# First two token tiles normed with gains read from PSUM in halves, two idle products for seven, another early order of weights and tokens

## The chip, the cores and the metric

The kernel runs on one core of one Trainium2 chip. The metric is the device time of one execution in microseconds (us), lower is better. A core has five engines that work side by side and meet at semaphores: TensorE (PE in the profile, with its weight loads as PEld), VectorE (DVE), ScalarE (ACT), GpSimd (POOL) and SyncE (SP), which here issues nearly all DMAs. Each engine takes its instructions in the order of its own queue.

## The reference

One encoder block on 1024 tokens of width 1024, with 16 meta tokens put ahead of them. What matters here is its first step: an RMS norm with a gain per column, and the projection of the normed tokens by `w_in`.

```python
def rms_norm(x, g):
    xf = x.astype(jnp.float32)
    y = xf * lax.rsqrt(jnp.mean(xf * xf, axis=-1, keepdims=True) + EPS)
    return (y * g.astype(jnp.float32)).astype(x.dtype)
...
    h = jnp.concatenate([meta, x], axis=1)
    for layer in range(DEPTH):
        h = h + mixer_block(rms_norm(h, norm_mix[layer]), w_in[layer], ...)
        h = h + swiglu(rms_norm(h, norm_ffn[layer]), w_ff_gate[layer], w_ff_up[layer], w_ff_down[layer])
    return rms_norm(h, norm_final)[:, N_META:]
```

Inside `mixer_block` come the projection `h @ w_in`, differential attention (branch A of the reference), windowed attention (branch B, with the parts `qb`, `kb` and `vb` of the projection), gates and an output product. `swiglu` is a feed-forward part of width 2816.

## The kernel before

All products are made in two parts: a float32 operand is split into a rounded high part and a low part (the rest), and a product is the sum of high by high, high by low and low by high. `split` (L114) makes the two parts of a weight: ACT copies the high part (L115), and DVE or POOL subtracts it from the weight (L116).

**Tokens.** `load_x(t)` loads tile t of 128 tokens (x0 to x7, and the 16 meta tokens, tile NT). `norm_x(t)` calls `normed` (L130): ACT squares the tile and sums it (L133), POOL makes the reciprocal root in two small steps (L121, the mean, and L122, a power), and DVE multiplies tile, root and gain in one SCALAR_TENSOR_TENSOR of 128x1024 (L139). `turn_x(t)` calls `transposed` (L142): eight PE transposes by 128 columns into two PSUM banks (L148), and for each bank an ACT copy to the high part `hT_hi` (L150) and a DVE subtraction to the low part `hT_lo` (L151).

**Gains.** The gain is one row of 1024 numbers. PE transposes and spreads it over the partitions into two PSUM banks of 512 columns (L456), and DVE copies both to the tile `gmix` in SBUF (L457).

**Projection.** `project_steps` (L205) multiplies one block of 128 weight columns with a chunk of tokens: 8 steps (one for each 128 rows of the weight) of 3 products (L218). For the first chunk `hi_first` puts the eight high by high products ahead. The first blocks are `kb` (column C_KB) and the first two blocks of `qb` (q0 and q1); they go through four chunks of 256 tokens, the last of `kb` with the 16 meta tokens. So chunk 0 needs x0 and x1, chunk 1 needs x2 and x3, and so on. Their weights are loaded ahead: `preload(C_KB)`, `preload(C_QB)` (tile `w_c`, L179) and `w_q1` (L464). `ensure(n)` calls `prep`, which splits the next weight in the list `order` and loads it first if it isn't there; KB's low part is made on POOL, those of q0 and q1 on DVE.

**Buffers.** x tiles and `w_q1` share the tag `btr` with four buffers, so that x3 waits for x0's product (L139), x4 for x1's, and x5 for the low part of `w_q1`. Raw weights `w_c` have two buffers, so that the third (VB) waits for KB's low part.

**Idle products.** Products of a tile of zeros into a bank that nobody reads stand in PE's queue: eight at the start (L448), six behind the gain (L460), seven behind the transposes of x1 (L473). The last seven use a second tile of zeros that DVE makes from x0's normed tile (L471).

**Order.** The program is written as one sequence, and a planner lays it out: it simulates the engines, and at each engine issues the earliest in the program of those instructions that are ready by its own model of durations. The order in each queue is then fixed. `tc.issue_after(ins)` makes all instructions of its block that are on the engine of `ins` follow `ins` in that queue, without a wait for its end. `advance(n)` issues n steps from the list `early`, which holds the first chunks' projections; what is not issued by the calls in between comes in a last `advance(100)`, and so stands last in priority, but fills PE wherever it is ready first.

```python
    with tc.issue_after(high.ins):        # high: the last hT_hi copy of x0
        ensure(1)
    load_x(3)
    high, _ = turn_x(1)
...
    early += [(p_kb, DC), (p_q0, DC), (p_q1, DC)]
    advance(E_STEPS)
    norm_x(3)
    turn_x(2)
    advance(E_STEPS)
    load_x(4)
    norm_x(4)
    _, low = turn_x(3)
```

Of the kernel before, what the change touches and what calls it, by code (L numbers as in the profile page):

```python
# [73 lines left out]
def encoder_block(ctx: ExitStack, tc: tile.TileContext, x, meta, norm_mix, w_in, lq1, lk1, lq2, lk2,  # L74
# [22 lines left out]
    def bank(p, tag, name, bufs):  # L97
        return p.tile([P, 512], F32, tag=tag, name=name, bufs=bufs)
# [26 lines left out]
    def row(p, src, n, name):  # L125
        t = p.tile([P, n], F32, name=name, bufs=1)
        nc.sync.dma_start(t, src.broadcast_to([P, n]))
        return t

    def normed(p, src, parts, gain, name, tag="xn", bufs=2, on_pool=False):  # L130
        xn = p.tile([P, D], F32, tag=tag, name=f"xn_{name}", bufs=bufs)
        ss = small.tile([P, 1], F32, tag="ss", name=f"ss_{name}")
        nc.scalar.activation(xn[:parts], src, AF.Square, accum_out=ss[:parts])  # L133
        r = rstd_of(ss[:parts], D, parts, f"rstd_{name}")
        if on_pool:
            nc.gpsimd.tensor_scalar(xn[:parts], src, r[:parts], 1.0, ALU.mult, ALU.mult)
            nc.gpsimd.tensor_tensor(xn[:parts], xn[:parts], gain[:parts], ALU.mult)
        else:
            nc.vector.scalar_tensor_tensor(xn[:parts], src, r[:parts], gain[:parts], ALU.mult, ALU.mult)  # L139
        return xn  # L140

    def transposed(pp, xn, parts, hi, lo, at, name):  # L142

        for b in range(2):
            pt = pp(f"ptn_{name}_{b}").rearrange("p (c t) -> p c t", c=4)
            for c in range(4):
                k = 4 * b + c
                nc.tensor.transpose(pt[:, c, :parts], xn[:parts, k * P:(k + 1) * P], ident[:parts, :parts])  # L148
            h = hi[:, 4 * b:4 * b + 4, at:at + parts]
            high = nc.scalar.activation(h, pt[:, :, :parts], AF.Copy)  # L150
            low = nc.vector.tensor_tensor(lo[:, 4 * b:4 * b + 4, at:at + parts], pt[:, :, :parts], f32(h), ALU.subtract)  # L151
        return high, low

    acon, close_acon = pool("acon", "right")
    hpool, close_hpool = pool("hpool", "right")
# [254 lines left out]
    def load_x(t):  # L410
        xts[t] = bpool.tile([P, D], F32, tag="btr", name=f"x_{t}", bufs=4)
        if t < NT:
            nc.sync.dma_start(xts[t], x[t * P:(t + 1) * P, :])
        else:
            nc.sync.dma_start(xts[t][:NM], meta)

    def norm_x(t):
# [4 lines left out]
        xns[t] = normed(bpool, xts.pop(t)[:parts], parts, gmix, f"a{t}", tag=tag, bufs=bufs)  # L422

    def turn_x(t):
        parts = P if t < NT else NM
        return transposed(lambda name: bank(psum1, ("bt", "bs")[t % 2], name, 2), xns.pop(t), parts, hT_hi, hT_lo, t * P, f"a{t}")

    def advance(n):
        while n > 0 and early:
            g, left = early[0]  # L430
            next(g)
            n -= 1
            if left == 1:
                early.pop(0)
            else:
                early[0] = (g, left - 1)


    zeros = bpool.tile([P, 512], BF16, tag="by1", name="zeros", bufs=2)
# [9 lines left out]
    pt = bank(psum1, "bt", "gain_t", 2)  # L449
    nc.tensor.transpose(pt[:, 0:DC], rows, ident[:DC, :DC])  # L450
    nc.vector.tensor_copy(gain_t, pt[:, 0:DC])
    for b in range(2):
        pt = bank(psum1, "bs", f"gain_{b}", 2)
        for c in range(4):
            k = 4 * b + c
            turned = nc.tensor.transpose(pt[:, c * P:(c + 1) * P], gain_t[:, k:k + 1].broadcast_to([P, P]), ident)  # L456
        nc.vector.tensor_copy(gmix[:, b * 512:(b + 1) * 512], pt)  # L457
    with tc.issue_after(turned.ins):
        for _ in range(6):
            nc.tensor.matmul(idle, zeros[:, 0:P], zeros, start=True, stop=True)  # L460
# [1 line left out]
    preload(C_QB)  # L462
    w_q1 = bpool.tile([P, D], F32, tag="btr", name="w_q1", bufs=4).rearrange("p (c n) -> p c n", n=P)
    nc.sync.dma_start(w_q1, w_in[:, C_QB + P:C_QB + 2 * P].rearrange("(c p) n -> p c n", p=P))  # L464
    norm_x(0)
    load_x(2)
    norm_x(1)
    xn0 = xns[0]
    high, _ = turn_x(0)
    zeros = bpool.tile([P, 512], BF16, tag="by1", name="zeros", bufs=2)  # L470
    nc.vector.tensor_scalar(zeros, xn0[:, 0:512], 0.0, None, ALU.mult)  # L471
    for _ in range(7):
        nc.tensor.matmul(idle, zeros[:, 0:P], zeros, start=True, stop=True)  # L473
# [1081 lines left out]
```

## Time and profile before

| what | value |
|---|---|
| time, median of 3 runs | 1433.33 us (1432.73 to 1434.84) |
| the profiled execution's own time | 1433.01 us |
| its span, first to last instruction | 1430.9 us |
| PE busy | 1420.2 us, 99% of the span |
| DVE, ACT, POOL busy | 909.7, 673.3, 468.1 us |
| mean granted PE clock | 0.999 |

Times in the views count from the span's start. A row of the timeline gives the start, the length, the engine, the line, the operation, `out<-in`, the shape, the count xN of like instructions in a row, and in brackets how long the engine was idle ahead of it and what ended that. A row of the chain of waits gives start, length and what the chain ran through. A row of the table of stretches gives a stretch, its length, and the busy time of each engine (with the number of instructions), the granted clock, the busy share of the DMA engines and the GB/s. A queue name with q (SPq, ACTq) marks the issuing of DMAs, and the listing of DMA issues gives the time from issue to landing.

### The profile page before, as it was taken

The page shows a single profiled execution, that of the slowest core. Times are in us where ns is not written, and L with a number is a line of the kernel's source. Part 1 is how long each engine was busy: PE and PEld are TensorE (multiplying, and loading weights), DVE is VectorE, ACT ScalarE, POOL GpSimd, SP SyncE. Part 2 cuts the span into 40 slices and gives each one's busy share as a digit, 9 for nine tenths or more (in the row PEclk, how much of TensorE's full clock was granted, in tenths as well). Part 3 has the DMA queues.
Part 4 walks back from the last instruction along what each step waited for, and adds up shares of the span by engine and source line. Part 5 has one row for each costly group of instructions (what it writes and reads, how often), then busy time and mean ns, then how long its engine had stood idle before and what let it go on. Part 6 is the DMA issues. An engine that isn't in the chain of part 4 may idle for free.

```text
span 1430.9 us, 20933 instructions
## 1 busy us (share of the span) xinstructions
PE 1420.2 (99%) x7287; PEld 1222.8 (85%) x7287; DVE 909.7 (64%) x1807; ACT 673.3 (47%) x1276; POOL 468.1 (33%) x462
## 2 busy tenths in 40 slices
PE   8999999999999999999999999999999999999998
PEld 7998899988999999888788888888888888888886
DVE  7366566428686868446878966655544553787566
ACT  6355555425455555455346654333333333444454
POOL 5133233222323232212503044554545552000442
PEclk9999999999999999999999999999999999999999
DMA  7344333381524251087431724433332333954344
GB/s 230 91 123 116 100 113 96 90 253 56 149 75 149 75 156 68 30 297 253 132 134 75 207 87 141 152 99 111 103 102 99 101 103 103 352 192 140 126 125 148
DMA packets 159018, 191.55 MB, mean 134 GB/s; under 512 B 16104, under 2 KB 103600, under 8 KB 158912
## 3 DMA queue, kind: packets, MB, share of 16 engines
q1 hardware_dynamic: 158320, 189.15, 41.7%
q8 instruction: 58, 0.95, 0.3%
q10 hardware_dynamic: 592, 1.05, 0.2%
q14 instruction: 48, 0.39, 0.1%
HBM read 129.67 MB, written 53.94 MB: 128 GB/s over the span
## 4 chain that ended last, share of the span: by engine, by line
PE 94%; DVE 2%; DMA 1%; ACT 1%; POOL 1%; issue 0%; DVEq 0%; ACTq 0%
PE pg L1318 29%; PE pd L1422 14%; PE pp_g L218 12%; PE aps L692 4%; PE po L1221 4%; PE apy L734 3%; PE pp_ka L218 3%; PE pp_va L218 3%; PE pp_qa L218 3%; PE pp_qb L218 3%; PE ppa L636 3%; PE apt L721 2%; PE bps L349 2%; PE po L1229 2%; PE bpy L389 1%; PE bpt L384 1%
## 5 line engine op out<-in xcount | busy, mean ns | idle before, releaser
L1318 PE MATMUL pg<-t,wop 128*128 128x512 f32 x1056 | 242.4, 389 | 0.0
L1318 PEld LDWEIGHTS pg<-t,wop 128*128 128x128 f32 x1056 | 198.2, 188 | 41.2
L1422 PE MATMUL pd<-ob,oa 128*128 128x512 f32 x924 | 209.6, 389 | 0.0
L116 POOL TENSOR_TENSOR wop<-wf,wop 128x512 fp32r<-128x512 f32 x114 | 154.2, 1353 | 162.0 <-ACT wop L115 148.5
L1422 PEld LDWEIGHTS pd<-ob,oa 128*128 128x128 f32 x924 | 173.4, 188 | 36.0
L1318 PE MATMUL pg<-b,wop 128*128 128x512 f32 x792 | 183.3, 389 | 0.0
L1318 PEld LDWEIGHTS pg<-b,wop 128*128 128x128 f32 x792 | 148.4, 188 | 30.7
L116 POOL TENSOR_TENSOR wl_c<-w_c,wh_c 128x1024 fp32r<-128x1024 f32 x32 | 77.3, 2415 | 131.5 <-ACT wh_c L115 122.2
L115 ACT ACTIVATE wop<-wf 128x512 fp32r<-128x512 f32 x128 | 80.8, 632 | 73.7 <-PE pg L1318 44.3
L703 ACT ACTIVATE as<-as,amn 128x1040 f32<-128x1040 f32 x64 | 74.5, 1165 | 73.6 <-DVE amn L698 73.5
L218 PE MATMUL pp_g<-hT_hi,wh_c 128*128 128x512 f32 x256 | 100.8, 394 | 0.0
L218 PE MATMUL pp_g<-hT_lo,wh_c 128*128 128x512 f32 x256 | 100.4, 392 | 0.0
L218 PE MATMUL pp_g<-hT_hi,wl_c 128*128 128x512 f32 x256 | 100.3, 392 | 0.0
L115 ACT ACTIVATE oa<-ra 128x512 fp32r<-128x512 f32 x77 | 48.7, 632 | 108.5 <-PE pd L1422 50.4
L692 PE MATMUL aps<-ak,aq 128*128 128x352 f32 (+1 forms) x384 | 92.7, 326 | 0.0
L116 POOL TENSOR_TENSOR oa<-ra,oa 128x512 fp32r<-128x512 f32 x27 | 34.9, 1294 | 168.6 <-ACT oa L115 167.2
L1095 DVE TENSOR_TENSOR s<-wf,wf 128x512 f32<-128x512 f32 x22 | 16.9, 769 | 111.4 <-DMA wf<-in_w_ff_up_dram 70.0
L692 PEld LDWEIGHTS aps<-ak,aq 128*128 128x128 f32 x384 | 69.6, 188 | 13.8 <-issue 0.2
L698 DVE CUSTOM_DVE_ANT_0 as<-aps,dist,amn 128x352 f32<-128x352 f32 (+1 forms) x128 | 71.4, 563 | 10.4 <-PE aps L692 8.3
L361 POOL TENSOR_SCALAR bs<-bs,bdn 128x432 f32<-128x432 f32 (+1 forms) x64 | 37.0, 597 | 112.6 <-DVE bdn L359 99.0
L698 DVE CUSTOM_DVE_ANT_0 as<-aps,dist,far_a 128x352 f32<-128x352 f32 x64 | 37.1, 580 | 42.2 <-PE aps L692 42.0
L706 POOL TENSOR_SCALAR as<-as,adn,neglam 128x1040 f32<-128x1040 f32 x32 | 38.9, 1215 | 75.6 <-DVE adn L704 75.6
(290 smaller groups left out, 3044.1 us busy)
## 6 DMA issues: line engine op xcount, KB each, us to landing
ra<-aop SPq DMA_DIRECT2D x77, 256.0 KB, 2.6
w_c<-in_w_in_dram SPq DMA_DIRECT2D x33, 512.0 KB, 3.9
wf<-in_w_ff_gate_dram SPq DMA_DIRECT2D x25, 512.0 KB, 3.8
wf<-in_w_ff_up_dram SPq DMA_DIRECT2D x25, 512.0 KB, 3.8
aop<-as SPq DMA_DIRECT2D x44, 256.0 KB, 2.0
aop<-c SPq DMA_DIRECT2D x33, 256.0 KB, 2.0
g_d<-gate_stage SPq DMA_DIRECT2D x32, 256.0 KB, 2.0
gt<-g_d SPq DMA_DIRECT2D x32, 256.0 KB, 3.8
```

The source lines that it names most:

```text
L115: high = nc.scalar.activation(hi, src, AF.Copy)
L116: lo_eng.tensor_tensor(lo, src, f32(hi), ALU.subtract)
L218: product = nc.tensor.matmul(ps[:, :n], a[:, c, :], b[:, c, at:at + n], start=(u == 0), stop=(u == 3 * DC - 1))
L636: nc.tensor.matmul(ps, w[:, a, j, :], src(j, b, tk), start=(j == 0 and n == 0), stop=(j == 3 and n == 2))
L692: nc.tensor.matmul(ps[:, :n], qs[m][:, t * P:(t + 1) * P], ks[m][:, vv, k0:k0 + n], start=(vv == 0), stop=(vv == 1))
L698: nc.vector.tensor_tensor_reduce(s[m][:, a:b], ps[:, a - k0:b - k0], far_by, slope, low, ALU.add, ALU.min, mn[:, m, i + j:i + j + 1])
L703: nc.scalar.activation(s[m][:, 0:L], s[m][:, 0:L], AF.Exp, bias=low, scale=-1.0, accum_out=dn[:, m:m + 1])
L706: (nc.gpsimd if t % 4 in COMBINE_POOL else nc.vector).tensor_scalar(s[1][:, 0:L], s[1][:, 0:L], dn[:, 1:2], neglam, ALU.mult, ALU.mult)
L734: nc.tensor.matmul(py[:, cols], v[:kp, a, k, :], at_[:kp, k, b, :], start=(k == 0 and j == 0), stop=(k == 8))
L1221: nc.tensor.matmul(sets_o[p][u], oa[:, a, u * P:(u + 1) * P], ob[:, b, :], start=(p in (1, 5) and j == 0 and k == 0), stop=(p in (2, 3) an ...
L1318: nc.tensor.matmul(ps, op[:, x, c, :], b[:, y, c, :], start=(p in (1, 5) and c == 0 and n == 0), stop=(p in (4, 2, 3) and c == 3 and n == ...
L1422: nc.tensor.matmul(ps[u], oa[:, a, u * P:(u + 1) * P], ob[:, b, :], start=(p in (1, 2, 5) and j == 0 and k == 0), stop=(p in (2, 3, 4) and ...
```

## The change

The spread gain stays in its two PSUM banks until x0 and x1 are normed: for these two tiles DVE makes two products of 128x512, each with its half of the gain read from PSUM. The copies to `gmix` stay, ahead of x0's products on DVE; all later tiles use `gmix`. KB's weight is split behind the square of x1 on ACT, ahead of x0's high part. The idle products behind x1 go, with their tile of zeros; two that use the first zeros stand behind the transposes of x0. The steps of q1's chunk 0 come behind the transposes of x2, x4's product comes behind x2's low parts on DVE, chunk 0 and the first two steps of `kb`'s chunk 1 are issued ahead of x5, and x4's transposes come behind them. `transposed` returns all high copies and the last transpose, `advance` its last product.

```diff
+    squares = []
+
     def normed(p, src, parts, gain, name, tag="xn", bufs=2, on_pool=False):
...
-        nc.scalar.activation(xn[:parts], src, AF.Square, accum_out=ss[:parts])
+        squares.append(nc.scalar.activation(xn[:parts], src, AF.Square, accum_out=ss[:parts]))
...
+        elif isinstance(gain, list):
+            for i, half in enumerate(gain):
+                cols = slice(i * 512, i * 512 + 512)
+                nc.vector.scalar_tensor_tensor(xn[:parts, cols], src[:, cols], r[:parts], half[:parts], ALU.mult, ALU.mult)
         else:
             nc.vector.scalar_tensor_tensor(xn[:parts], src, r[:parts], gain[:parts], ALU.mult, ALU.mult)
...
+    gain = []
     for b in range(2):
         pt = bank(psum1, "bs", f"gain_{b}", 2)
+        gain.append(pt)
         for c in range(4):
             k = 4 * b + c
             turned = nc.tensor.transpose(pt[:, c * P:(c + 1) * P], gain_t[:, k:k + 1].broadcast_to([P, P]), ident)
-        nc.vector.tensor_copy(gmix[:, b * 512:(b + 1) * 512], pt)
+        copied = nc.vector.tensor_copy(gmix[:, b * 512:(b + 1) * 512], pt)
...
-    norm_x(0)
+
+    with tc.issue_after(copied.ins):
+        norm_x(0, gain)
     load_x(2)
-    norm_x(1)
-    xn0 = xns[0]
-    high, _ = turn_x(0)
-    zeros = bpool.tile([P, 512], BF16, tag="by1", name="zeros", bufs=2)
-    nc.vector.tensor_scalar(zeros, xn0[:, 0:512], 0.0, None, ALU.mult)
-    for _ in range(7):
-        nc.tensor.matmul(idle, zeros[:, 0:P], zeros, start=True, stop=True)
-
-    with tc.issue_after(high.ins):
+    norm_x(1, gain)
+    with tc.issue_after(squares[-1].ins):
         ensure(1)
+    _, _, turned = turn_x(0)
+    with tc.issue_after(turned.ins):
+        for _ in range(2):
+            nc.tensor.matmul(idle, zeros[:, 0:P], zeros, start=True, stop=True)
     load_x(3)
-    high, _ = turn_x(1)
+    highs, _, _ = turn_x(1)
     q1_h, q1_l = (bpool.tile([P, DC, P], F32R, tag=tag, name=f"{tag}_q1", bufs=1) for tag in ("wh", "wl"))
-    with tc.issue_after(high.ins):
+
+    with tc.issue_after(highs[-1].ins):
         ensure(2)
         high = split(q1_h, q1_l, w_q1, nc.vector)
...
-    early += [(p_kb, DC), (p_q0, DC), (p_q1, DC)]
+
+    def behind(steps, other):
+        for _ in range(DC):
+            with tc.issue_after(other.ins):
+                product = next(steps)
+            yield product
+
+    early += [(p_kb, DC), (p_q0, DC)]
     advance(E_STEPS)
     norm_x(3)
-    turn_x(2)
+    _, low, turned = turn_x(2)
+
+    early.append((behind(p_q1, turned), DC))
     advance(E_STEPS)
     load_x(4)
-    norm_x(4)
-    _, low = turn_x(3)
+    with tc.issue_after(low.ins):
+        norm_x(4)
+    _, low, _ = turn_x(3)
     early += [(p_kb, DC), (p_q0, DC), (p_q1, DC)]
-    advance(E_STEPS)
+
+    product = advance(3 * DC)
     load_x(5)
     norm_x(5)
-    turn_x(4)
+    with tc.issue_after(product.ins):
+        turn_x(4)
     advance(E_STEPS)
```

More of the change, by code (lines that the diff above doesn't have):

```diff
@@ L147, in transposed @@
                 k = 4 * b + c
-                nc.tensor.transpose(pt[:, c, :parts], xn[:parts, k * P:(k + 1) * P], ident[:parts, :parts])
+                turned = nc.tensor.transpose(pt[:, c, :parts], xn[:parts, k * P:(k + 1) * P], ident[:parts, :parts])
             h = hi[:, 4 * b:4 * b + 4, at:at + parts]
-            high = nc.scalar.activation(h, pt[:, :, :parts], AF.Copy)
+            highs.append(nc.scalar.activation(h, pt[:, :, :parts], AF.Copy))
             low = nc.vector.tensor_tensor(lo[:, 4 * b:4 * b + 4, at:at + parts], pt[:, :, :parts], f32(h), ALU.subtract)
-        return high, low
+        return highs, low, turned
     acon, close_acon = pool("acon", "right")
@@ L421, in norm_x @@
         tag, bufs = ("vt", 1) if i % 3 == 2 else ("bs", 2)
-        xns[t] = normed(bpool, xts.pop(t)[:parts], parts, gmix, f"a{t}", tag=tag, bufs=bufs)
+        xns[t] = normed(bpool, xts.pop(t)[:parts], parts, gain or gmix, f"a{t}", tag=tag, bufs=bufs)
     def turn_x(t):
@@ L430, in advance @@
             g, left = early[0]
-            next(g)
+            product = next(g)
             n -= 1
```

4 lines of the change are left out of this document (3 added, 1 removed).

## The prediction

> **What bounds the kernel now.** I read the page first, for the share of each engine, then the table of stretches, for where PE is idle.
>
> ```profile
> PE 1420.2 (99%) x7287; PEld 1222.8 (85%) x7287; DVE 909.7 (64%) x1807; ACT 673.3 (47%) x1276; POOL 468.1 (33%) x462
> 0.00:26.00 26.00, 22.02 (x149) 17.16 (x150) 17.02 (x22) 16.48 (x28) 13.77 (x46) 1.00 0.89 282
> 26.00:50.00 24.00, 24.00 (x203) 23.69 (x203) 18.43 (x35) 10.53 (x25) 4.20 (x8) 1.00 0.37 95
> 50.00:1400.00 1350.00, 1349.46 (x6831) 1161.91 (x6831) 852.67 (x1711) 631.35 (x1194) 443.68 (x396) 1.00 0.42 131
> ```
>
> PE bounds the kernel. Behind 26 us it is idle for 0.54 us in 1374 us; in the first 26 us it is idle for 3.98 us, and part of its 22.02 busy us are idle products. The change edits this stretch alone. Since PE is full behind it, every us by which useful products get ahead there should come off the end, and no more can be won than the idle time and the idle products that the stretch holds. The chain of waits tells what the first products wait for, and what stops PE at 24 us.
>
> ```profile
> 5.63 1.30 DVE gmix L457 x2
> 7.13 1.30 DVE xn_a L139
> 8.48 0.67 PE ptn_a L148 x4
> 10.26 0.94 ACT wh_c L115
> 11.20 0.97 ACT hT_hi L150 x2
> 15.91 6.96 DMA x<-in_x_dram
> 22.96 1.15 ACT xn_a L133 x2
> 24.11 0.49 ACT hT_hi L150
> 24.62 0.70 DVE hT_lo L151
> 25.37 1.69 PE pp_kb L218 x12
> ```
>
> Two things are to be seen. First, the head is one serial chain through DVE (gain copies, then x0's product), PE's transposes and ACT, and on ACT the split of KB's weight (10.26) stands between the high parts of x0 and x1. Second, the square of x5 waits for its load, which lands at 15.91 + 6.96 = 22.87, and x3's high part stands behind that square on ACT. Chunk 1 needs x3.
>
> The timeline of PE gives the rest of the head and the second stop.
>
> ```profile
> 1.17 3.35 PE L448 MATMUL idle<-zeros 128*128 128x512 bf16 x8 [1.17 <-DVE zeros L440]
> 5.87 1.46 PE L460 MATMUL idle<-zeros 128*128 128x512 bf16 x6
> 11.21 1.67 PE L473 MATMUL idle<-zeros 128*128 128x512 bf16 x7
> 12.53 1.30 PE L218 MATMUL pp_kb<-hT_hi,wh_c 128*128 128x256 f32 x8
> 13.66 0.28 PE L218 MATMUL pp_kb<-hT_lo,wh_c 128*128 128x256 f32 x1
> 20.35 1.03 PE L148 MATMUL ptn_a<-ident,xn_a 128*128 128x128 f32 x8
> 21.14 0.37 PE L218 MATMUL pp_qb<-hT_lo,wh_q 128*128 128x256 f32 x1
> 23.06 1.14 PE L148 MATMUL ptn_a<-ident,xn_a 128*128 128x128 f32 x8
> 24.64 0.39 PE L218 MATMUL pp_kb<-hT_hi,wh_c 128*128 128x256 f32 x1 [0.44 <-ACT hT_hi L150]
> 36.62 2.87 PE pp_kb L218 x24
> ```
>
> The last row is the chain's: 24 products in 2.87, so 0.12 each where nothing waits. Eight transposes take 21.14 - 20.35 = 0.79 of PE's queue. So behind the transposes at 23.06 a product could start at 23.85; it starts at 24.64, and the third of chunk 1 at 25.37 instead of 24.64 + 0.24 = 24.88. The second stop costs 0.79 + 0.49 = 1.28 us.
>
> **The head, step by step.** These are the rows of the other engines.
>
> ```profile
> 6.04 0.56 POOL L122 TENSOR_TENSOR rstd_a<-rstd_a,neg_half 128x1 f32<-128x1 f32 x1
> 7.30 1.53 POOL L122 TENSOR_TENSOR rstd_a<-rstd_a,neg_half 128x1 f32<-128x1 f32 x1
> 8.87 1.29 DVE L139 SCALAR_TENSOR_TENSOR xn_a<-x,rstd_a,gmix 128x1024 f32<-128x1024 f32 x1 [0.45 <-POOL rstd_a L122]
> 16.60 1.28 DVE L139 SCALAR_TENSOR_TENSOR xn_a<-x,rstd_a,gmix 128x1024 f32<-128x1024 f32 x1 [0.71 <-POOL rstd_a L122]
> 18.61 1.28 DVE L139 SCALAR_TENSOR_TENSOR xn_a<-x,rstd_a,gmix 128x1024 f32<-128x1024 f32 x1 [0.72 <-POOL rstd_a L122]
> 28.74 1.28 DVE L151 TENSOR_TENSOR hT_lo<-ptn_a,hT_hi 128x512 fp32r<-128x512 f32 x2
> 29.44 0.55 POOL L122 TENSOR_TENSOR rstd_a<-rstd_a,neg_half 128x1 f32<-128x1 f32 x1
> 21.81 0.48 DVE L245 SCALAR_TENSOR_TENSOR qk_stage<-pp_qb,qbs,qk_stage 128x256 fp32r<-128x256 f32 x1
> 10.41 2.60 DVE L151 TENSOR_TENSOR hT_lo<-ptn_a,hT_hi 128x512 fp32r<-128x512 f32 x4
> 11.28 2.39 POOL L116 TENSOR_TENSOR wl_c<-w_c,wh_c 128x1024 fp32r<-128x1024 f32 x1 [2.44 <-ACT wh_c L115]
> 14.67 1.21 DVE L116 TENSOR_TENSOR wl_q<-w_q,wh_q 128x1024 fp32r<-128x1024 f32 x1
> 9.17 1.09 ACT L150 ACTIVATE hT_hi<-ptn_a 128x512 fp32r<-128x512 f32 x2 [2.23 <-PE ptn_a L148]
> 1.63 1.06 SPq L179 DMA_DIRECT2D w_c<-in_w_in_dram  x2
> w_c<-in_w_in_dram SPq DMA_DIRECT2D x1, 512.0 KB, 5.6
> 5.78 1.45 SPq L413 DMA_DIRECT2D x<-in_x_dram  x1
> x<-in_x_dram SPq DMA_DIRECT2D x1, 512.0 KB, 6.8
> ```
>
> *Halves from PSUM.* No row shows this product. From below a half of 1.30 is 0.65; from above, the same operation from PSUM at 256 columns took 0.48, and its slope to 1.30 at 1024 gives 0.75 at 512. I take 0.68, nearest to the 2.60 / 4 = 0.65 of L151, which reads PSUM at this size. x0's product waits no longer for the copies' writes (0.20 between 6.93 and 7.13), though it stays behind them in the queue; its root is there at 6.60. So the halves end at 7.6 and 8.3 where the whole ended at 8.43, and x0's transposes start at 7.65 instead of 8.48, the second four at 8.35.
>
> *x1's root.* The power at 7.30 took 1.53 beside DVE's product of two SBUF tiles (7.13 to 8.43), and 0.56 or 0.55 otherwise, also beside a DVE subtraction that reads PSUM (28.74). With the gain in PSUM the root should be there at 7.86, not 8.83; x1's product then waits only for DVE, 8.3 to 9.65 (before 8.87 to 10.16). If POOL is still held until 8.3, the power ends at 8.86 and x1 comes 0.5 later.
>
> *KB's split on ACT.* The weight lands at 1.63 + 5.6 = 7.23, and ACT is idle for 2.23 ahead of 9.17. So the 0.94 of the split go to 7.25 to 8.3, in that gap, and the low part on POOL ends at 8.3 + 2.39 = 10.7. x0's high parts follow at 8.3 and 8.9. The cover is thin: if the weight landed at 8.2, x0 would wait, us for us.
>
> *Two idle products for seven.* Seven hold PE for 1.46 (0.21 each by the 1.67 of seven against 1.46 of six). kb's first product started right behind them at 12.53, although the first half of x1's high parts was there at about 11.7. Two cost 0.43 ahead of x1's transposes, which can then start at 9.1 (x1's first half is there at 9.0). Its high parts on ACT come at 9.65 to 10.2 and 10.2 to 10.75, where the second ended at 12.17. The first four products can run at 10.25, the other four from 10.75, all eight by 11.25, against 13.66 before: 2.4 us ahead. The low end is a first product at 10.75 with the 1.13 that the eight took before, by 11.9, so 1.8; with POOL held, 1.3.
>
> *What is late next.* DVE's low parts of x0 and x1 run from 9.65, each 0.65 and the third not before 10.25: 12.2 at the latest. kb's remaining products take 16 x 0.12 to 13.2 and find POOL's part done; q0 lasts to 16.1, its weight split on ACT until 11.7 and on DVE until 13.4, q1's until 14.6. q1 must now wait behind x2's transposes. x2 lands at 5.78 + 6.8 = 12.6, unmoved; square about 1.0, and of the root's two steps the first is held by DVE's split to 14.6, the power takes 0.6 more, product 1.3: 16.4. Against 16.1 that is 0.3 lost on PE, with q1's 24 products queued behind. I take 2.4 - 0.3 = 2.1 for the head, 1.3 to 2.4.
>
> **The second stop.** Chunk 1 is now due at 16.4 + 24 x 0.12 + 2 x 0.79 = 20.9. x3's product on DVE follows x2's by 2.0 us (16.60, 18.61), held by POOL as before, 18.4; transposes and ACT give its high parts by 20. x4's product, now queued behind x2's low parts, still stands ahead of x3's low parts (1.3 + 0.65), which come at about 21.1: 0.2 lost. If the square of x5 doesn't stand ahead of x3's high part, 1.28 - 0.2 = 1.1 is won; between -0.3 and 1.28 otherwise. x4's transposes behind six products of chunk 1 change no count: 0.79 is paid later, and chunk 2, which needs x4, is 8 us off.
>
> The moved loads: KB's buffer comes free 3 us earlier, so VB's load enters SP's queue ahead of x5; x5's own buffer comes free at 14.6 instead of 15.9. DVE also loses the tile of zeros. All this lies beside PE.
>
> **Sum.** 2.1 + 1.1 = 3.2 us off the profiled execution's 1433.0 us: 1429.8. The median of the runs is 0.3 above that execution, so I forecast 1430.1 us. Own range 1.9 to 4.1 (idle time of 3.98, less 1.17 of start, with the 1.3 to 1.46 of idle products): 1429.2 to 1431.4.
>
> One rule speaks against this. By the Trainium skill (TensorE: Matmul & The Clock Gate, Part 4, PE-mode transpose) transposes do not count as PE activity for the clock gate, and by its table "Why this matters for your kernels" idle gaps above about 3 us bring the half clock back. By that rule the sum would be that of the clock case below. Here 7.33 to 11.21 held only transposes, 3.9 us, and the seven products behind it still took 0.21 each, so the trace does not show that; no run here shows the gap with two products in it.
>
> **Rivals.**
>
> *Clock.* The first eight idle products took 3.35 us, 0.42 each, twice the later 0.21. If PE came out of the transposes at that pace for as long, half of 3.35 = 1.7 would be lost: 1431.8. The stretch with few products shrinks from 3.9 us to two of about 1.3 and 1.2, which speaks against.
>
> *x5 still between x2 and x3.* The planner goes by its own durations and may leave ACT's order as it is. x5's load starts at 14.6 and takes 5.6 to 6.96: lands at 20.2 to 21.6; the third product came 25.37 - 22.87 = 2.5 behind, so 22.7 to 24.1, while 24.6 is what now corresponds (25.37 less the 0.79 of x4's transposes). Won in all: 0.5 to 1.9, middle 1.2, 1432.1.
>
> *x5 ahead of both (slower).* If the square of x5 stands ahead of x2's high parts too, two more of 0.5 come behind it: third product 3.5 behind the landing. From a landing at 21.1 the change loses. If the load lands as late as now, 22.87, because VB's and the next weight's 1 MB go ahead of it, it comes at 26.4: 1.8 lost, 1435.1. For: DMA is at 0.89 in this stretch. Against: today x2 goes first.
>
> *The plan behind.* One order is laid out for the whole program from one simulated clock, so later queues may be dealt anew though the edits are early. PE's 0.54 idle leaves nothing to win there; a new order could cost some us. I put it at 1428.6 to 1437, without a row that names a place, middle 1432.8.
>
> **How the numbers follow.** Forecast 0.66, x5 between 0.12, x5 ahead of both 0.08, clock 0.05, plan 0.09. What a measurement of this kernel can tell from no change is 0.2%, 2.9 us, so faster means below 1430.5, inside the forecast's own range: four fifths of the forecast, 0.53, and 0.02 of the last case give 0.55. Slower is above 1436.2: a third of x5 ahead of both (a landing later than now) and half of the plan case, 0.08. The rest, 0.37, is within. The range runs from 1428.8 (the own range and 0.4 for the spread of runs) to 1433.2, through the clock and x5 between; beyond lie x5 ahead of both and part of the plan case, and some of the forecast below.
>
> **What would show it.** Right: x0's product as two of about 0.68, first transposes near 7.7; the power for x1 at 0.56; KB's split ahead of x0's high parts; kb's first product before 11; no stop above 0.5 us at chunk 1; the stretch from 26 on as busy as now. Wrong: a power of 1.5 us, a first idle product or product of kb at twice its pace, ACT waiting for a DMA ahead of x2's or x3's high parts, q1 waiting more than 1 us for x2, or new idle time of PE behind 50 us.

## Result and profile after

The changed kernel took 1437.32 us, the median of 17 runs (1433.41 to 1439.16), beside 1433.33 us for the kernel before: a ratio of 1.0025, interval 1.0017 to 1.0032. It is slower by 4.0 us, where 3.2 us less had been forecast, and it lies above the range. The profiled execution took 1436.73 us, its span 1434.8.

The page's row of engines and the table of stretches of the changed kernel:

```profile
PE 1422.1 (99%) x7282; PEld 1224.7 (85%) x7282; DVE 909.5 (63%) x1808; ACT 674.3 (47%) x1276; POOL 463.9 (32%) x462
```

```profile
0.00:26.00 26.00, 20.77 (x131) 15.95 (x131) 15.40 (x22) 16.05 (x27) 10.97 (x46) 1.00 0.82 266
26.00:50.00 24.00, 23.85 (x191) 23.69 (x191) 19.36 (x36) 11.10 (x24) 6.74 (x8) 0.93 0.41 108
50.00:1400.00 1350.00, 1348.98 (x6838) 1161.73 (x6837) 850.64 (x1711) 631.03 (x1192) 437.77 (x395) 1.00 0.41 131
```

Again PE is full behind 26 us, and again the loss lies ahead of 50 us. PE is idle for 5.23 us in the first 26 (3.98 before), and from 26 to 50 the granted clock is 0.93 (1.00 before): PE is busy there, but with fewer products (191 against 203). At VB's first product, where both orders have done the same work, the change is 3.0 us behind (57.8 against 54.8 us); at the end of the span 3.9.

The head, on the timelines of POOL, ACT, DVE and PE:

```profile
7.14 0.56 POOL L122 TENSOR_TENSOR rstd_a<-rstd_a,neg_half 128x1 f32<-128x1 f32 x1
7.62 1.06 ACT L115 ACTIVATE wh_c<-w_c 128x1024 fp32r<-128x1024 f32 x1 [0.84 <-DMA w_c<-in_w_in_dram]
7.59 2.71 DVE L144 SCALAR_TENSOR_TENSOR xn_a<-x,rstd_a,gain 128x512 f32<-128x512 f32 x4
5.23 1.72 PE L467 MATMUL gain<-ident,columns 128*128 128x128 f32 x8 [0.26 <-DVE columns L460]
8.39 1.32 PE L156 MATMUL ptn_a<-ident,xn_a 128*128 128x128 f32 x8
11.26 1.25 PE L226 MATMUL pp_kb<-hT_hi,wh_c 128*128 128x256 f32 x8 [0.18 <-ACT hT_hi L158]
12.35 0.28 PE L226 MATMUL pp_kb<-hT_lo,wh_c 128*128 128x256 f32 x1
```

The four halves take 2.71 / 4 = 0.68 each, x1's power 0.56, and KB's split stands ahead of x0's high parts, as forecast. The power is nearly over (7.70) when the halves start (7.59), so these rows alone don't show it beside them; the kernel with x5's square moved, below, does: there the halves run from 6.78, and the power at 7.40 took 0.56. The eight products of `kb` are done at 12.35, 1.3 us ahead of before (13.66). So the head did get faster. Now the second stop, on ACT, PE and SP:

```profile
19.49 1.09 ACT L158 ACTIVATE hT_hi<-ptn_a 128x512 fp32r<-128x512 f32 x2
23.74 1.06 ACT L136 ACTIVATE xn_a<-x 128x1024 f32<-128x1024 f32 x1 [3.16 <-DMA x<-in_x_dram]
24.79 1.07 ACT L158 ACTIVATE hT_hi<-ptn_a 128x512 fp32r<-128x512 f32 x2
21.74 0.28 PE L226 MATMUL pp_qb<-hT_hi,wl_q 128*128 128x256 f32 x1
25.42 0.38 PE L226 MATMUL pp_kb<-hT_hi,wh_c 128*128 128x256 f32 x1 [3.40 <-ACT hT_hi L158]
26.15 0.39 PE L226 MATMUL pp_kb<-hT_lo,wh_c 128*128 128x256 f32 x1 [0.22 <-DVE hT_lo L159]
8.68 0.36 SPq L574 DMA_DIRECT2D lam_in<-in_lambda_q_dram  x1
11.19 1.66 SPq L421 DMA_DIRECT2D x<-in_x_dram  x2
15.09 2.94 SPq L421 DMA_DIRECT2D x<-in_x_dram  x2
31.57 0.41 SPq L421 DMA_DIRECT2D x<-in_x_dram  x1
```

ACT's order is x2's high parts (19.49), x5's square (23.74), x3's high parts (24.79), the same three as before. x5's load starts at 15.09 (before 15.91) and lands at 23.74 (before 22.87). PE is through with chunk 0 at 21.86 (21.74 and 0.12), 1.2 us ahead of before (23.06), and then stands still until 25.42. The third product of chunk 1 comes at 26.15, where 21.86 + 0.24 = 22.10 was possible: a stop of 4.05 us against 1.28. The rows of SP show two side effects: the four small loads `lam_in` now stand ahead of x3's and x4's (11.19, against 8.45 and 10.19 before), since the second tile of zeros, which held one of their two buffers, is gone; and x7's load comes at 31.57 (before 21.92), behind the writes of the first stages of `kb` and `qb`.

What follows the stop is seen in the table of stretches of 1 us (behind the length: busy PE, PEld, DVE, ACT, POOL, then the granted clock, the DMA share and the GB/s):

```profile
22.00:23.00 1.00, 0.02 (x1) 0.00 (x0) 1.00 (x1) 0.00 (x0) 0.00 (x0) 1.00 0.87 296
24.00:25.00 1.00, 0.00 (x0) 0.00 (x0) 0.00 (x0) 1.00 (x3) 0.03 (x1) 1.00 0.47 127
26.00:27.00 1.00, 0.85 (x7) 0.85 (x8) 1.00 (x2) 1.00 (x3) 0.02 (x1) 1.00 0.25 66
27.00:28.00 1.00, 1.00 (x8) 1.00 (x6) 1.00 (x5) 0.50 (x2) 0.92 (x3) 0.52 0.48 122
29.00:30.00 1.00, 1.00 (x7) 1.00 (x6) 1.00 (x2) 0.21 (x1) 0.00 (x0) 0.50 0.51 129
30.00:31.00 1.00, 1.00 (x9) 1.00 (x8) 0.80 (x2) 0.00 (x0) 0.00 (x0) 0.78 0.31 79
```

and in PE's timeline of the same time:

```profile
26.85 1.72 PE L156 MATMUL ptn_a<-ident,xn_a 128*128 128x128 f32 x8
28.59 0.41 PE L226 MATMUL pp_kb<-hT_lo,wh_c 128*128 128x256 f32 x1
30.29 0.36 PE L226 MATMUL pp_qb<-hT_hi,wh_c 128*128 128x256 f32 x1
```

From 27.0 to 30.4 us PE has half its clock (in the four stretches from 27 to 31 it has lost 0.48, 0.50, 0.50 and 0.22 of full speed). x4's transposes (26.85; the next product starts at 28.23) hold its queue for 1.38 (0.79 before), and the eight products from 28.59 to 30.29 take 0.21 each (0.12 before): 0.59 + 0.74, and 0.24 for the product between them and the one behind, about 1.6 us. The account up to VB's first product closes within 0.2: 1.2 won, 4.05 - 1.28 = 2.8 lost at the stop, 1.6 lost to the clock, together 3.2; measured are 3.0.

### The profile page after: what moved, and what is told of

Same layout as the page of the kernel before. It is cut to its first block, busy times and chain, and to the rows that moved or that the text cites. A ratio compares the mean times of both kernels' runs of the same rounds, so it can differ in the third digit from the quotient of the medians.

```text
span 1434.8 us, 20929 instructions
## 1 busy us (share of the span) xinstructions
PE 1422.1 (99%) x7282; PEld 1224.7 (85%) x7282; DVE 909.5 (63%) x1808; ACT 674.3 (47%) x1276; POOL 463.9 (32%) x462
## 3 DMA queue, kind: packets, MB, share of 16 engines
q10 hardware_dynamic: 592, 1.05, 0.2%
## 5 line engine op out<-in xcount | busy, mean ns | idle before, releaser
L116 POOL TENSOR_TENSOR wop<-wf,wop 128x512 fp32r<-128x512 f32 x114 | 150.4, 1320 | 165.4 <-ACT wop L115 156.9
L359 DVE CUSTOM_DVE_ANT_0 bs<-bps,tbx,nsink 128x432 f32<-128x432 f32 (+1 forms) x64 | 38.7, 627 | 41.1 <-PE bps L357 28.1
```

What stands on the lines that cost most here:

```text
L116: lo_eng.tensor_tensor(lo, src, f32(hi), ALU.subtract)
L359: nc.vector.tensor_tensor_reduce(st[:, r, :W], ps[:, :W], tb, 2.0 ** -(4 * g + r + 1), nsink[:, 4 * g + r:4 * g + r + 1], ALU.add, ALU.min ...
```

## Experiments

In all of them `loads[t]` holds the DMA of tile t, and a time stands beside the kernel before as it ran on the same chip (medians 1433.26 to 1433.77). Two theories stood at the start. *Late loads:* x5 and x3 are late because their loads stand behind the small ones on SP. *Place on ACT:* x5's square ahead of x3's high parts turns any lead into a wait.

**The two halves of the change.** One kernel has the new head with the order of before behind it, the other the old head with the new order.

> The changed kernel's head alone: gains from PSUM in halves, KB's split early on ACT, two idle products, but the later order (q1, x4, x5) as before. lam_in's loads still stand ahead of x3's and x4's, as there is no second tile of zeros. Theory 5 (arrival): PE is ready for chunk 1 about 1.3 us earlier, x5 lands at 23.5 to 24, a little later than before; the third product of chunk 1 stays at 25.5 to 26.5, the stop grows to about 3 us and in most executions the clock falls: 1434 to 1437, not faster than before. By the prediction the head alone would give 2.1 off, 1431.2.

> The kernel before with the changed kernel's later order alone: q1 behind x2's transposes, x4's product behind x2's low parts, chunk 0 and two steps of chunk 1 issued ahead of x5, x4's transposes behind them. The head, the seven idle products and the second tile of zeros stay, so x3's and x4's loads come ahead of most of lam_in's. Theory 5 (arrival): x5 lands near 22.9 as before, x4's transposes no longer fill the wait, so the stop is about 2 us and its end stays: 0.8 lost by the transposes that come later, 1434. If x7's load, which now stands behind the writes of the first kb and q0 chunks, makes PE wait near 40 us, as with both edits above, 1 to 2 us more, 1435 to 1436. By the prediction this part alone would win 1.1 us, 1432.2.

The head alone took 1435.60 us (1.0012, 1.0003 to 1.0021), the order alone 1435.97 (1.0019, 1.0010 to 1.0028). Either half loses. PE's rows of the head alone:

```profile
23.05 1.25 PE L156 MATMUL ptn_a<-ident,xn_a 128*128 128x128 f32 x8 [1.60 <-DVE hT_lo L159]
25.72 0.58 PE L226 MATMUL pp_kb<-hT_hi,wh_c 128*128 128x256 f32 x1 [1.42 <-ACT hT_hi L158]
```

With the head alone x5's square waits until 24.04 (before: 22.87), PE stops twice, and the half clock lasts from 25 to 32 us. With the order alone there are stops of 0.71 and 1.85 us, for x3's high and low parts, and the half clock lasts from 25.6 to 29.0. So the loss isn't the new order's alone: by the medians each half brings more than half of it by itself, the head 2.2 us and the order 2.6, and the two don't add up. (The profiled execution of the head alone took 1438.31 us, 2.7 more than its median.)

**The small loads back behind x4's.** Edit of the changed kernel:

```diff
+    with tc.issue_after(loads[4].ins):
         for i, v in enumerate((lq1, lk1, lq2, lk2)):
             nc.sync.dma_start(lam_in[:, i, :], v.broadcast_to([P, HD]))
```

> The changed kernel, with the four loads of lam_in issued behind the load of x4 on SP's queue; nothing else is edited. Theory 1 (loads): without the second tile of zeros lam_in's buffer is free early, its loads stand ahead of those of x3 and x4, these start at 11.2 instead of 8.45 and 10.19, the DMA engines are nearly idle from 11 to 13, and x5 lands late. Then x3's load starts near 9 here, x5 lands at about 22 instead of 23.7, PE's stop of 3.4 us ahead of chunk 1 shrinks by about 1.8, the clock keeps its full rate, and the time falls by about 3 us to 1434. Theory 2 (ACT's order alone): x5's landing hardly moves, since its own load starts no earlier; time within 1 us of 1437. Theory 3 (the plan behind 50 us is at fault): no change.

1436.57 us (1.0018, 1.0009 to 1.0027). x3's and x4's loads start at 8.79 and 9.90, and x5's at 14.62, and it helps nothing:

```profile
23.82 1.06 ACT L136 ACTIVATE xn_a<-x 128x1024 f32<-128x1024 f32 x1 [5.33 <-DMA x<-in_x_dram]
25.51 0.58 PE L226 MATMUL pp_kb<-hT_hi,wh_c 128*128 128x256 f32 x1 [3.98 <-ACT hT_hi L158]
```

x5 lands at 23.8 all the same, and PE, ahead by more, waits longer. The theory of late loads falls as the sole cause: starting x5's load 0.5 us sooner (14.62, against 15.09) did not land it sooner.

**x5's square behind x3's high parts.**

```diff
-    load_x(5)
-    norm_x(5)
+    load_x(5)
+    with tc.issue_after(highs[-1].ins):   # the last high copy of x3
+        norm_x(5)
```

> The changed kernel, with the square of x5 (and its other ACT work) queued on ACT behind x3's high parts; the loads keep the changed kernel's order. Theory 2 (ACT's order): x3's high parts were held by a square that waits for a load, so PE's stop of 3.4 us goes but for about 0.4, the half clock behind it goes (1.5 us), and the time falls by about 5 us to 1432, though x5 lands as late as before. Theory 1 (loads): x3 itself is late by its load, so most of the stop stays; at most 1 us is won, 1436. Theory 3 (the plan behind 50 us): no change.

1434.82 us (1.0012, 1.0003 to 1.0021): more than half of the loss is gone. Now the square waits for its load behind x3's high parts, where PE doesn't need it:

```profile
20.12 2.32 ACT L158 ACTIVATE hT_hi<-ptn_a 128x512 fp32r<-128x512 f32 x4
25.21 1.06 ACT L136 ACTIVATE xn_a<-x 128x1024 f32<-128x1024 f32 x1 [2.77 <-DMA x<-in_x_dram]
```

But x3 itself is late, since its load stands behind the small ones: PE waits 0.74 for x3's product and 1.80 for its low part, and runs at the half clock from 24.5 to 28.

**Both edits.**

> The changed kernel with both edits: lam_in's loads behind x4's, and the square of x5 behind x3's high parts on ACT. If ACT's order alone makes the stop, this equals the second edit alone, 1432. If the late loads matter beside it (x4 and x5 late for chunk 2), this is 0.5 to 1 us better, 1431. By the prediction's sum (3.2 off 1433.3) it would be 1430.1, since the stop is gone and the head stands.

1433.95 us (1.0004, 0.9995 to 1.0013), level with before. Rows of ACT, PE and SP:

```profile
21.00 1.09 ACT L158 ACTIVATE hT_hi<-ptn_a 128x512 fp32r<-128x512 f32 x2 [2.28 <-PE ptn_a L156]
21.97 1.06 ACT L136 ACTIVATE xn_a<-x 128x1024 f32<-128x1024 f32 x1
22.60 0.39 PE L226 MATMUL pp_kb<-hT_lo,wh_c 128*128 128x256 f32 x1 [0.44 <-DVE hT_lo L159]
40.36 1.06 PE L156 MATMUL ptn_a<-ident,xn_a 128*128 128x128 f32 x8 [1.13 <-DVE xn_a L146]
31.09 2.05 SPq L422 DMA_DIRECT2D x<-in_x_dram  x1
```

x5's square (21.97) follows x3's high parts and waits for nothing. The early stop is down to 0.44, the clock stays at 1.00, and PE has 23.64 busy us in the first 26 (22.02 before). But from 26 to 50 it is busy for 22.00 of 24: x7, loaded at 31.09 behind the stage writes, makes PE wait from 40 us on. The 1.6 us that the first stretch won are lost in the second.

**The clock held.** Fourteen idle products stand where the changed kernel stops.

```diff
-    product = advance(3 * DC)
+    product = advance(3 * DC - 2)
+    with tc.issue_after(product.ins):
+        for _ in range(14):
+            nc.tensor.matmul(idle, zeros[:, 0:P], zeros, start=True, stop=True)
+    product = advance(2)
```

> The changed kernel with 14 more idle products in PE's queue between q1's chunk 0 and kb's chunk 1, 3.0 us at 0.21 each, so inside the stop of 3.4 us, which they neither shorten nor lengthen. Theory 4 (clock): the stop lets the granted clock fall to a half for about 3.4 us; with the idle products it stays at 1.00 from 27 to 31, and the time falls by 1.5 to 2 us to about 1435.5. If the clock's fall came from something else than the stop, or cost nothing, the time stays at 1437.

1436.66 us (1.0019, 1.0010 to 1.0028). The clock stays at 1.00, so the half clock does come from PE's idleness at the stop. But the median is only 0.7 us below the changed kernel's, and the intervals overlap, so that the time fell is not shown. In this run PE waits 0.82 and 0.20 for x7 and the meta tokens (41.33, 43.31); that the slow clock of the changed kernel had covered these waits is argued, not shown.

**Why x5 lands late.** Third theory, *arrival:* VB's and QA's weights (1 MB), loaded ahead of x5, share the DMA engines with it; their busy share is 1.01, 1.15 and 1.05 in the three stretches of 2 us from 16 to 22 us (1.06, 1.14 and 1.00 in the kernel before). A first attempt held those two loads until behind x6's load, in both kernels, by a wait at the place where the program makes them:

```diff
-        nc.sync.dma_start(w, ...)
+        with tc.issue_after(loads[6].ins) if col in (C_VB, C_QA) else nullcontext():
+            nc.sync.dma_start(w, ...)
```

> The changed kernel, with the loads of the next two weights (VB and the first of qa, 1 MB in all) queued on SP behind x6's load; they had stood ahead of x5's. ACT's order is untouched: the square of x5 still stands ahead of x3's high parts. Theory 5 (arrival): in the changed kernel and with lam_in's loads moved, x5 landed at 23.7 to 23.8 whether its load began at 15.1 or 14.6, because that 1 MB goes ahead of it; so the head's gain only lengthens PE's stop. Then x5 lands 2 to 3 us earlier here, at about 21, the stop shrinks from 3.4 us to about 1, the half clock goes, and the time falls by about 4 us to 1433. Theory 6 (x5 is bound by its own issue or by the stage writes): x5 lands at 23 or later still, time 1436 to 1437.

> The kernel before, with the loads of VB and of the first block of qa queued on SP behind x6's load, and nothing else. Theory 5 (arrival): x5 lands near 20.5 instead of 22.87, and the stop of 1.28 us ahead of chunk 1 goes: 1432.0, faster by 1 to 1.3 us. Theory 6: no change, 1433.3.

These took 1458.17 and 1454.95 us (1.0167 and 1.0153), a miss in the edit: the planner then put the loads behind all stage writes, at 72.1 and 69.5 us, and PE stood still for some 16 us between 50 and 80 us, with a mean granted clock of 0.74 from 50 to 90 us behind these stops. Their first 26 us still tell something: x5's square waited for no DMA, and in the kernel before the early stop was gone (PE busy for 23.11 us, not 22.02). The second attempt makes the loads right behind x6's, and in the changed kernel issues x5's and x6's ahead of chunk 0's products:

```diff
+    load_x(5)
     load_x(6)
+    with tc.issue_after(loads[6].ins):
+        preload(C_VB)
+        preload(C_QA)
```

> The changed kernel with the loads of VB's and QA's weights (1 MB) put behind x6's load on SP's queue, ahead of the writes of kb's and qb's stages; ACT's order is not touched. Arrival theory (x5's transfer shares the engines with that 1 MB, so it lands near 23.8 us whenever it starts, and its square holds up x3's high part): x5's square runs by 20 to 21 us, the stop ahead of chunk 1's first product shrinks from 4.1 us to about 1, the clock holds at 1.00 between 25 and 31 us, and the time is about 1434. Rival (x5 is late because its own load is issued late): its square still waits until about 23.8 and the time stays at 1437.

> The kernel before with the same move of the loads of VB's and QA's weights behind x6's load. Arrival theory: x5's square runs by 20 to 21 us, the stop of 1.28 us ahead of chunk 1's first product goes, and the time is about 1432.0 (1.3 us below the kernel before). Rival: the stop stays and the time is 1433.3; or VB's weights are then late for their first product, and it is above.

The changed kernel so edited took 1436.89 us (1.0027, 1.0017 to 1.0036), no better; the kernel before 1433.02 (0.9995, 0.9986 to 1.0004), where 1432.0 was expected. Rows of the first, whose profiled execution took 1438.39 us, on ACT, DVE and PE:

```profile
20.50 1.08 ACT L136 ACTIVATE xn_a<-x 128x1024 f32<-128x1024 f32 x1
21.54 1.10 ACT L158 ACTIVATE hT_hi<-ptn_a 128x512 fp32r<-128x512 f32 x2
23.57 1.28 DVE L146 SCALAR_TENSOR_TENSOR xn_a<-x,rstd_a,gmix 128x1024 f32<-128x1024 f32 x1 [0.44 <-POOL rstd_a L122]
24.77 1.28 DVE L159 TENSOR_TENSOR hT_lo<-ptn_a,hT_hi 128x512 fp32r<-128x512 f32 x2
25.50 0.58 PE L226 MATMUL pp_kb<-hT_lo,wh_c 128*128 128x256 f32 x1 [2.80 <-DVE hT_lo L159]
```

That the 1 MB delays x5 is shown: behind it x5's load takes 4.8 us (14.19 to 19.0) in the first and 4.3 (16.25 to 20.5) in the second, and x5 is there when ACT comes to it. In the kernel before the stop of 1.28 us is gone, but 0.91 us is lost instead at VB's first product:

```profile
55.26 0.44 PE L218 MATMUL pp_vb<-hT_hi,wh_c 128*128 128x384 f32 x1 [0.91 <-DVE qk_stage L242]
```

How late the 1 MB makes x5 is not settled by it, since the same 1 MB stood ahead of x5 in the kernel before, too: there the load took 6.96 us, in the changed kernel 8.65, and with the small loads moved 9.2.

In the edited changed kernel a stop stays, from another queue: on DVE, x5's product (23.57, waiting for its root) stands ahead of x3's low parts (24.77), behind x4's product (21.85), and of the stop of 2.80 us it accounts for 1.65 (23.12 to 24.77). That order is this run's own, where x5's load is issued ahead of chunk 0's products; in the changed kernel x3's first low part (25.40) stands ahead of x5's product (26.01). So what the changed kernel would take in its own order with x5 on time is not shown.

**x7 and meta ahead of the writes.** Added to the run with both edits: the loads of x5, x6, meta and x7 are issued ahead of chunk 0's products, and q0's and q1's writes behind x7's load. A second kernel also has VB's and QA's weights behind x6.

> The run with both moves (the four small loads behind x4's, x5's square behind x3's high part), and the loads of x7 and of the table meta put ahead of most writes of kb's and qb's stages. Theory that the 2 us which that run lost between 26 and 50 us are x7's late load: the waits of x7's transposes near 40 us go and the time is about 1432.0, below the kernel before by 1.3. Rival (it is the writes' own queueing or something later): no change against 1434.0.

> As the last, with VB's and QA's weights behind x6's load as well. If the arrival of x5, its place on ACT, and x7's load are the three places where the head's gain went, no stop over 0.7 us is left ahead of 50 us, the clock holds, and the time is 1431 to 1431.5, about 2 us below the kernel before. Rival (the gain is given back later than 50 us): about 1433.3.

1433.20 us (1.0000, 0.9991 to 1.0009) and 1434.30 (1.0006, 0.9998 to 1.0015). In the first, PE is busy for 24.00 of 24 us from 26 to 50, and VB's first product comes at 52.5, 2.3 us ahead of before. So x7's load was the wait of 2 us. Yet branch A's first scores come at 317.1, against 317.2: the lead is lost in between. ACT's and PE's rows of that run:

```profile
75.58 1.06 ACT L115 ACTIVATE wh_c<-w_c 128x1024 fp32r<-128x1024 f32 x1 [3.57 <-DMA w_c<-in_w_in_dram]
87.09 0.74 PE L398 MATMUL bpy<-btr,vb 128*128 128x512 f32 x2 [1.39 <-DVE btr L396]
```

and the corresponding row of ACT in the kernel before:

```profile
75.39 1.06 ACT L115 ACTIVATE wh_c<-w_c 128x1024 fp32r<-128x1024 f32 x1 [1.10 <-DMA w_c<-in_w_in_dram]
```

The split of VA's first weights starts at the same time in both, since their load stands on SP behind stage writes (issued at 71.4 in both); everything behind it on ACT and DVE waits, and at 87.09 so does PE. In the second kernel 0.82 us go at VB's first product, which comes at 54.3.

**VA's first weights sooner.** With a third buffer for raw weights, the load goes ahead of a block of stage writes:

```diff
-        w = raw_w[col] = wpool.tile([P, DC, P], F32, tag="w", ..., bufs=2)
+        w = raw_w[col] = wpool.tile([P, DC, P], F32, tag="w", ..., bufs=3)
...
     norm_x(NT)
+    with tc.issue_after(loads[7].ins):
+        preload(C_VA)
```

> The run with the small loads, x5's square, and the loads of x7 and meta moved, now with three buffers for raw weights, and VA's first weights loaded ahead of the writes of chunk 1's stages (about 43 us) instead of behind those of chunk 3's (71.4 us). Theory that the lead is given back there: ACT's split of these weights does not wait until 75.5 us, PE's wait of 1.39 us at branch B's first values (87 us) goes, branch A's first scores start 1.5 us or more ahead of the kernel before (317.2 us), and the time is 1431 to 1431.8. Rival (later work fills up in any case): PE waits elsewhere ahead of 320 us, and the time stays at 1433.2.

> The same move in the run that also puts VB's and QA's weights behind x6's load. By the theory 1432 to 1433 (it still waits 0.8 us ahead of VB's first product, 1434.3 before the move); by the rival 1434.3.

> The kernel before with three buffers and the same early load. By the theory no change that can be measured (1433.3), since PE does not wait there between 26 and 320 us; where the early load itself, or the third buffer later on, is worth something, it is below 1432.5.

1444.13 us (1.0070, 1.0057 to 1.0084), 1443.57 (1.0066, 1.0053 to 1.0080) and 1465.60 (1.0225, 1.0211 to 1.0240). The third buffer costs far more than it could bring: PE waits 8.2 us at the first output product of branch B (`ppa`, 632.85), far behind the place in question, and in the kernel before VB's load also fell behind the writes (70 us, PE idle for 11.7 us). The first of them also moves VB's and QA's loads, right behind x4's. Behind the wait of 8.2 us the granted clock is 0.83 from 620 to 650 us, which is half clock for some 10 us. Up to 320 us the first run still answers: VA's split starts at 65.61, the wait of 1.39 us is gone, and branch A's first scores come at 316.3, 0.9 us ahead of before. The same load was then issued from ACT's queue, with two buffers:

```diff
-        nc.sync.dma_start(w, ...)
+        q = nc.scalar if col == C_VA else nc.sync
+        q.dma_start(w, ...)
```

> The run with the small loads, x5's square, and the loads of x7 and meta moved, with the load of VA's first weights issued from ACT's queue at about 52 us instead of from SP's at 71.4. Theory that the lead of 2.3 us is given back at those weights: PE's wait of 1.39 us at 87 us goes, branch A's first scores start at 316 us or sooner (before: 317.2), and the time is 1431.3 to 1432.2. Rival (later work fills up in any case): the wait turns up elsewhere and the time stays at 1433.2.

> The same for the run that also puts VB's and QA's weights behind x6's load. By the theory 1432.5 to 1433.5 (it still waits 0.8 us ahead of VB's first product); by the rival 1434.3.

> The kernel before with the same load on ACT's queue. By the theory no change that can be measured (1433.3): PE has no wait between 26 and 320 us that this load could end sooner.

1432.40 us (0.9993, 0.9984 to 1.0001), 1435.07 (1.0006, 0.9998 to 1.0015) and 1433.23 (0.9998, 0.9989 to 1.0007). Rows of the first, on ACT's queue and on PE:

```profile
54.03 0.43 ACTq L188 DMA_DIRECT2D w_c<-in_w_in_dram  x1
64.58 1.06 ACT L115 ACTIVATE wh_c<-w_c 128x1024 fp32r<-128x1024 f32 x1 [0.42 <-PE pp_vb L227]
306.99 0.50 PE L227 MATMUL pp_g<-hT_hi,wh_c 128*128 128x512 f32 x1 [1.28 <-ACT gate_stage L671]
```

The split comes at 64.58, PE has no wait from 50 to 100 us, and the lead lasts: KA's first product comes at 96.7 (before 98.8), the first gate product at 294.7 (before 296.8), 2.1 us ahead. Then it goes: by branch A's first scores, at 316.7 (before 317.2), 1.6 us of it is lost, 1.28 of them at the gate product shown; another 1.18 goes at 387.29, at a product of the scores that waits for the load of K. So the place named at 75 us was right, and the rival was right about the end: the next waits fill up. (The profiled execution took 1435.10 us, 2.7 more than the median; where others lose their lead is not shown.) This is the best of all kernels by its median, 1.3 us below the kernel before, with an interval that holds 1; 4.9 us below the changed kernel, 1437.32. That it beats the kernel before is not shown.

## Why the prediction was wrong

*The head* came in its pieces, and at the low end of the sum: 1.3 us where 2.4 was taken. The eight products of `kb` were done at 12.35, not 11.25. Over the runs with this head the first product came between 10.35 and 11.50, where 10.25 to 10.75 was forecast. Part of the difference lies ahead of the edit: the eight gain transposes took 1.09 to 1.97 us in those runs, 1.72 in the profiled one. But the term was also too large by itself. Half a us of it was to come from x1's power, 1.53 us before, and that duration goes with DVE's product starting ahead of the power, which the old head does not always bring. In four of six profiles with the old head the power took 0.56, and DVE's product started behind the power's start (power 7.35, product 7.46 in the kernel before with the weights behind x6). With equal gain transposes the new head has `kb`'s eight products done 1.5 us sooner than these (13.40 in the order alone against 11.88 with the small loads moved, 1.09 both; 13.87 against 12.35, 1.71 and 1.72), and 2.1 sooner only than the execution with 1.53 (13.66 against 11.53). q1 behind x2's transposes cost 0.05 us (17.15 to 17.20), where 0.3 was costed.

*The second stop* is the step that failed. Its sentence was "If the square of x5 doesn't stand ahead of x3's high part, 1.28 - 0.2 = 1.1 is won; between -0.3 and 1.28 otherwise." It did stand ahead, and otherwise was worth -2.8. The forecast worked out from its own rows that chunk 1 would be due 3 us sooner and did not set that against x5's landing; a landing as late as 22.87, with the 1 MB as its reason, stands only in the rival *x5 ahead of both*, beside an order that did not come. The rival *x5 still between x2 and x3* had the mechanism and the wrong landing: it added the old transfer's 5.6 to 6.96 us to the new start, 14.6. The start came at 15.09 and the transfer took 8.65. The runs show that sharing the engines with VB's and QA's 1 MB makes the load slow: 4.3 and 4.8 us with that 1 MB behind it, 7 to 11 with it ahead. What sets the time within 7 to 11 us stays open: the landing was at 22.9 in before, 23.7 in the changed kernel, 23.8, 24.0 and 25.2 with the small loads moved, the head alone and the square moved, and at 22.0 or sooner with both edits. With 23.74 in place of 20.2 to 21.6 that rival's own arithmetic gives 23.74 + 2.5 = 26.2 for the third product (measured: 26.15) and a loss. On top come some 1.6 us of half clock behind the stop, which no term of the sum or of this rival had. Its chance of 0.12 was too small as well: no row spoke for a new order on ACT.

*The clock rival* (0.05) was priced in the head, where nothing of it came, and not at the stop it follows from. Of the rule of the Trainium skill that the prediction weighed (TensorE: Matmul & The Clock Gate, "Why this matters for your kernels"), the stop of 3.40 us and the half clock behind it are an instance. On the other, Part 4 on transposes, these runs don't decide: in the head alone two stops of 1.60 and 1.42 us with nothing but eight transposes in between were followed by 6.8 us of half clock, but with the order alone stops of 0.71 and 1.85 us, with two products in between, were followed by 3.4 us of it. The gap in the head of before, 3.9 us with nothing but transposes, brought none.

*The moved loads* were "beside PE". The small loads' buffer was noticed only as DVE's tile of zeros that goes, not as what had held those loads back; x7's and meta's loads, x7's 10 us later, made PE wait for nothing in the changed kernel and for 2 us as soon as the stop was gone.

*The plan behind* didn't come: the queues are the same behind the early part.

*"Every us by which useful products get ahead there should come off the end"* failed for a reason of its own, which the runs show. PE's 99% hides that at 75, 87 and 307 us other engines run with little slack. A lead of 2.3 us at VB's first product ended at 317 us as 0.1 us; with VA's load moved a lead of 2.1 at 295 us was 0.5 there.

What stays open: what sets x5's landing among the other loads, what the last waits, at 307 and 387 us, would give if K's load and the gate's stage came earlier, and how much of the 0.9 us by which the profiled change falls further behind after 55 us is the edit's and not the run's. That 0.9 is lost behind 317 us: the change is 2.9 behind at branch A's first scores (320.1 against 317.2) and 3.9 at 716 us.

## What to carry to other kernels

Where a queue's order is fixed, look for the instruction that stands in front of the critical one and waits for a load: making the critical side earlier only lengthens that wait. Don't take the load's landing as its new start plus its old time: here that gave 20.2 to 21.6, and it landed at 23.74. A longer stop can be paid twice: here stops of 2.5 to 4 us, in one piece or in two, brought PE back at half its clock, which cost about 1.6 us more in the changed kernel. An engine that is 99% busy is no proof that a lead lasts to the end: follow the next loads and splits that start at a fixed time.

## What the runs showed of the hardware

The half clock began between 24.3 and 27 us and lasted about 3.4 us (27.0 to 30.4 in the changed kernel, 25.5 to 28.9, 24.5 to 27.9 and 25.6 to 29.0 in the kernels with the small loads moved, x5's square moved, and the new order alone) or twice that (25.1 to 31.9 for the head alone, 24.3 to 31.2 with the weights behind x6); behind longer stops it lasted longer, some 10 us behind the 8.2 us wait with the third buffer; stops of 0.71 and 1.85 us with two products in between sufficed. The Trainium skill (TensorE: Matmul & The Clock Gate, Part 1) tells of a free-running window of about 3.4 us; these lengths agree. By such a window the same stop would cost a different amount from run to run, and the changed kernel's 17 runs do go with the granted clock: 1433.41 us at 1.000, 1433.99 at 0.999, 1435.55 to 1437.95 at 0.998, 1436.96 to 1439.16 at 0.997, 1437.47 to 1438.07 at 0.996. The start of the full clock moves in the same way: the gain transposes took 1.09, 1.31, 1.72 and 1.97 us in executions of the same head.

x5's load of 512 KB took 4.3 and 4.8 us with the 1 MB of weights behind it (both kernels with the weights behind x6), and with that 1 MB ahead of it 6.96 us in before, 8.65 in the changed kernel and 9.2 with the small loads moved, where it started 0.5 us sooner (14.62 against 15.09) and landed no sooner. POOL's power took 1.53 and 1.47 us where DVE's product of two SBUF tiles had started ahead of it (before, and before with VA's load on ACT's queue), and 0.56 in the four other profiles of the old head, where the product started behind it.
